# Decays of two heads in one tile, and in-block matmuls that alternate between the column halves of the array

## The chip, the cores and the metric

The kernel runs on one core of a Trainium2 chip. The metric is the device time of one execution in microseconds (us). TensorE (PE) multiplies matrices, VectorE (DVE), ScalarE (ACT) and GpSimd (POOL) work elementwise, and SyncE (SP) mainly issues DMA transfers. Each engine takes its instructions in the order of its own queue and waits on semaphores for the others.

## What is computed

The reference is one residual block over 512 tokens and 2048 channels: a root-mean-square norm, one wide projection, a retention branch (8 heads), a Mamba-2 branch (SSD, 64 heads of 64 channels in 8 groups), a gated merge, an output projection and a final norm. The change lies in the scan of the SSD branch. Cut to that:

```python
acum = jnp.cumsum(ac, axis=1)
seg = acum[:, :, None] - acum[:, None, :]
decay = jnp.exp(jnp.where(causal, seg, -jnp.inf))
cb = jnp.einsum('blgn,bsgn->blsg', cc, bc)
y = jnp.einsum('blsg,blsgh,bsghp->blghp', cb, decay, xc)
y = y + jnp.einsum('blgn,bghpn->blghp', cc, state) * jnp.exp(acum)[..., None]
```

`cb` belongs to a group and is shared by its 8 heads; `decay` belongs to a head. The product with `decay`, summed over the tokens `s` of a block, is what this text calls the in-block sum.

## The kernel before

The 512 tokens (T) are four blocks (TB) of 128 (P). Most of the time goes to the projections: `unit` makes 256 output columns for all tokens. Its float32 operands are split into two parts of reduced precision (`split`, L150 and L151), so that each product takes three matmuls (L202 to L204). SP loads the weights `wf` (L216), DVE forms sums of weight blocks (L219 to L222), ACT makes the high part `whi`, DVE the low part `wlo`. PE accumulates in the PSUM banks `pb`.

The scan's stage starts at L557. For each of 8 groups there is one unit for B and C, then twice (`jj`): a unit for x, a unit for z, the scan of two feature blocks (`e` = 0, 1), and a unit of the merge gates (`gates`, L582). A feature block is 128 channels, that is two heads. For each one:

- x is transposed and scaled (L621 to L627, `xd`, `xl`), the states at the block ends are formed (L630 to L639, `S`);
- for each of the two heads, SP loads the head's cumulative decay `A_d`, the same 512 numbers for all 128 partitions, into a tile `L` of two buffers (L644). ACT makes the decays with four Relus, one for each token block (L646), and one exponential (L648). DVE multiplies with `CB`, the group's masked `cb` (L649). Four matmuls (L651) form the in-block sums;
- these four use 64 weight columns each. The first head's result goes to PSUM partitions 0 to 63 and the second's to 64 to 127, so each head uses one column half of the array;
- three matmuls bring in the states (L655), and DVE and ACT finish `y` (L657 to L667).

The matmuls of L621, L630, L651 and L655 are float32 and leave two records each in the trace; those of L202 to L204 leave one. An unbroken run of L651 matmuls on PE is called a block below.

The order on each engine's queue is not that of the text. A scheduler of the framework (L819) lists the whole program with a model of times, so PE's scan matmuls stand among the projection matmuls of the next units.

Of the kernel before, what the change touches and what calls it, by code (L numbers as in the profile page):

```python
# [8 lines left out]
F32 = mybir.dt.float32  # L9
F32R = mybir.dt.float32r  # L10
I32 = mybir.dt.int32
AF = mybir.ActivationFunctionType
ALU = mybir.AluOpType
# [3 lines left out]
P = 128  # L17
T = 512
# [13 lines left out]

# columns of the constant array
C_ID, C_TRI, C_ONE, C_FREQ, C_END = 0, 128, 256, 384, 386


def _parts_of_inverse_two_pi():
    """1/(2 pi) as a sum of 12-bit pieces, high to low."""
    digits = 0.15915494309189533576888376337251436203445964574045644874766734405889
    from fractions import Fraction  # L40

    # 1/(2 pi) to 200 bits by Machin's formula
    def atan_inv(n, bits):
        one = 1 << bits
        term = one // n
        total, k, sign = term, 1, 1
        while term:
            term //= n * n
            k += 2
            sign = -sign  # L50
            total += sign * (term // k)
        return total

    bits = 240
    pi = 4 * (4 * atan_inv(5, bits) - atan_inv(239, bits))
    inv = Fraction(1 << bits, 2 * pi)
    assert abs(float(inv) - digits) < 1e-15
    parts = []
    for i in range(5):
        step = Fraction(1, 1 << (14 + 12 * i))  # L60
        n = inv // step
        parts.append(float(n * step))
        inv -= n * step
    return parts


def constants():
# [7 lines left out]
    for h in range(NH):  # L75
# [5 lines left out]

# A 256-row by 256-column block of weights B times a 256-feature by 512-token block of
# activations A.  Rows of A are the token halves, its columns the two feature tiles; t1 is
# half 1 and t0 is half 2, the odd weight tile is column 1 and the even one column 2.
# Activation slots: 0 A21, then A12-(A21+A22-A11), 1 A11, 2 A22, 3 A12, 4 A21+A22,
# 5 A21+A22-A11, 6 A21-A11.
# Weight slots: 0 B12, then B22+B11-B12, 1 B11, 2 B22, 3 B21, 4 B11-B12, 5 B22-B12,
# 6 B21-(B22+B11-B12).
# A product is (bank, half of the bank, weight slot, activation slot).
# SEVEN: Strassen's products in Winograd's form.  EIGHT: the block product with A21 as  # L90
# A11+(A21-A11), on the weights as they are.
SEVEN = (((0, 0, 1, 1), (1, 0, 3, 3), (1, 1, 0, 5)),
# [4 lines left out]
         ((2, 0, 0, 6), (2, 0, 2, 2), (2, 1, 2, 3)))  # L97
# EIGHT in two passes, the second half of the tokens first, each with banks of its own.
PASSES = ((((0, 0, 1, 1), (0, 1, 0, 1)), ((1, 0, 3, 3), (1, 1, 2, 3))),
# [12 lines left out]
class InOrder:  # L112
    """An engine whose instructions issue in the order of the program."""

# [15 lines left out]
def hybrid_block(tc, A, out):  # L130
# [15 lines left out]
    def att_tile():  # L146
        return att.tile([P, T], F32, name="att")
# [4 lines left out]

    # ------------------------------------------------ products with the weights
    def combined(f, eng):
# [7 lines left out]
    def operands(i, f):  # L162
        """The seven activation operands of feature pair i from its raw slots 0-3 in f."""
        combined(f, POOL if i in FORM_POOL else DVE)
# [12 lines left out]
    def load_operands(forms, src, last=None):  # L177
        """Operands of 2048 features of a DRAM array [features, T]; the last pair may be on chip."""
        H = []
# [9 lines left out]
    def products(H, parts, pt, groups, PE=PE, after=None):  # L189
        """The products of groups, for 256 columns of weights, into the banks pt: parts are  # L190
        DRAM arrays [2048, n], side by side."""
        started, ws = set(), []
# [46 lines left out]
    def unit(H, parts, alt=False, plain=False):  # L239
        """W^T A for 256 columns of weights as two tiles [128, T], feature-major."""  # L240
        nb = 3 if plain else 4
# [21 lines left out]

    # ---------------------------------------------------------------- stage 0
    cc = cst.tile([P, C_END], F32, name="cc")
# [8 lines left out]

    # scratch
    yr_d = dp.tile([D, T], F32, name="yr_d")
# [12 lines left out]
    def inverse_root(dst, ps, y, z, n, DVE=DVE, ACT=ACT):  # L289
        """dst = (ps / n + eps) ** -0.5 for sums in PSUM; a Newton step makes it exact.  # L290
        y, z: room for one tile each."""
        ACT.activation(y, ps, AF.Abs_reciprocal_sqrt, scale=1.0 / n, bias=eps)
# [4 lines left out]

    # forms of the activations before they are split: A8 and B8 serve other ends between
    bg_ctx = ExitStack()
# [15 lines left out]
    with tc.tile_pool(name="st0", bufs=1) as st:  # L315
        def early(tag):
            """Room of an operand that is not yet there."""
            return hp.tile([P, 7 * 256], F32, name=f"e_{tag}", tag=tag)

        # the order of the arithmetic here is that of the text  # L320
        pe, act, dve, pool = (InOrder(tc, e) for e in (PE, ACT, DVE, POOL))
        raw = [early(f"hl{i}")[:, :2 * T].rearrange("p (r t) -> p r t", r=2) for i in range(NP)]
        wdt = early("hh7")[:, :KD * SH].rearrange("p (k c) -> p k c", k=KD)
        for i, x in enumerate(raw):
            SP.dma_start(out=x, in_=rows(A["xT"], i))
            if i == 0:
                SP.dma_start(out=cc, in_=A["consts"])
        # brings the table in ahead
        act.activation(rstd[:, :1], eps, AF.Abs_reciprocal_sqrt)
# [27 lines left out]

        # the normalized activations
        fs, hs, H = {}, {}, []
# [25 lines left out]
    def rotary_tables(positions, x):  # L385
        """cos and sin of the angles, which are rounded as the reference rounds them, then
        counted in turns and reduced exactly; x is room for four tiles."""
        turn, a1, a2, ki = (x[:, i, :] for i in range(4))
# [34 lines left out]
    def step_sizes(v, pool):  # L423
        """dt = softplus(h w + bias), the cumulative decays in blocks of 128 tokens."""
        u, w, s, s2 = (v[:, i, :].rearrange("p (c h) -> p c h", c=TB) for i in range(4))
# [8 lines left out]
        for tb in range(TB):  # L434
            DVE.scalar_tensor_tensor(u[:, tb, :], pt[:, tb * SH:(tb + 1) * SH], rstd[:, tb:tb + 1], dtb,
                                     op0=ALU.mult, op1=ALU.add)
        # softplus: max(u, 0) + log1p(exp(-|u|)), log1p(w) = 2 atanh(w / (2 + w))
        DVE.tensor_scalar(w, u, -1.0, None, op0=ALU.mult)
# [36 lines left out]

    # -------------------------------------------------------------- retention
    with tc.tile_pool(name="ret", bufs=1) as rp:
# [3 lines left out]
        for h in range(NH):  # L481
            # the decays stay where the gate comes later
            dec = sg[:, 0, :]
# [72 lines left out]

    # -------------------------------------------------------------------- SSD  # L557
    with tc.tile_pool(name="ssd", bufs=1) as sp:
        # conv taps and bias; D
        cw = sp.tile([P, 48, 5], F32, name="cw")  # L560
# [12 lines left out]
        def conv(x, j, dst):  # L573
            """causal convolution over tokens and SiLU of one feature block."""
            ACT.activation(dst, x, AF.Identity, scale=cw[:, j, 3:4], bias=cw[:, j, 4:5])
# [13 lines left out]
        for g in range(NG):  # L589
# [14 lines left out]
            for jj in range(2):  # L604
# [5 lines left out]
                for e in range(2):  # L610
# [5 lines left out]
                    for i in range(2):  # L616
                        SP.dma_start(out=E[i * 64:(i + 1) * 64, :], in_=E_d[h0 + i, P:].partition_broadcast(64))
                    # x token-major, scaled by dt, and by dt and the decay to the block's end
                    ps = att_tile()
# [14 lines left out]
                    for c in range(1, TB - 1):  # L634
                        for i in range(2):
# [3 lines left out]
                                                     op0=ALU.mult, op1=ALU.add)  # L639
                    pi = att_tile()  # L640
                    for i in range(2):
                        # decay from s to l within a block; s > l is zeroed by CB
                        L = sp.tile([P, TB, P], F32, name="L", bufs=2)
                        SP.dma_start(out=L.rearrange("p c l -> p (c l)"), in_=A_d[h0 + i].partition_broadcast(P))  # L644
                        for c in range(TB):
                            ACT.activation(L[:, c, :], L[:, c, :], AF.Relu, scale=-1.0,  # L646
                                           bias=At[:, c, h0 + i:h0 + i + 1])
                        ACT.activation(L, L, AF.Exp, scale=-1.0)  # L648
                        DVE.tensor_tensor(L, L, CB, op=ALU.mult)  # L649
                        for c in range(TB):  # L650
                            PE.matmul(pi[i * 64:(i + 1) * 64, c * P:(c + 1) * P], xd[:, c, i, :], L[:, c, :],  # L651
                                      start=True, stop=True)
# [19 lines left out]

    # --------------------------------------------------- branch projections
    with tc.tile_pool(name="br", bufs=1) as bp:
# [41 lines left out]

    # ----------------------------------------------------- output projection
    with tc.tile_pool(name="fin", bufs=1) as fp:
# [16 lines left out]

        # the last two feature blocks, the odd one first, half of the tokens after the other
        t = xo[NP - 1]
# [85 lines left out]
```

## Time and profile before

| | |
|---|---|
| median of 3 runs | 2796.94 us |
| lowest, highest | 2796.71, 2799.17 us |
| span of the profiled execution | 2798.7 us (no other time is given for it) |
| PE busy | 2738.8 us, 98% of the span |
| DVE busy | 2380.8 us, 85% |
| ACT busy | 1333.9 us, 48% |
| in-block matmuls L651, busy | 59.5 us, 512 records |

The span runs from the first to the last instruction of one execution. Busy time is the union of an engine's instructions; matmuls overlap each other in the pipeline, so a record's duration (0.28 us) is longer than the step from one start to the next. "Idle before" is the time in which an engine had nothing to do ahead of the instructions of a group, and what ended it. PEld is the load of weights into the array.

### The profile page before, as it was taken

The page shows a single profiled execution, that of the slowest core. Times are in us where ns is not written, and L with a number is a line of the kernel's source. Part 1 is how long each engine was busy: PE and PEld are TensorE (multiplying, and loading weights), DVE is VectorE, ACT ScalarE, POOL GpSimd, SP SyncE. Part 2 cuts the span into 40 slices and gives each one's busy share as a digit, 9 for nine tenths or more (in the row PEclk, how much of TensorE's full clock was granted, in tenths as well). Part 3 has the DMA queues.
Part 4 walks back from the last instruction along what each step waited for, and adds up shares of the span by engine and source line. Part 5 has one row for each costly group of instructions (what it writes and reads, how often), then busy time and mean ns, then how long its engine had stood idle before and what let it go on. Part 6 is the DMA issues. An engine that isn't in the chain of part 4 may idle for free.

```text
span 2798.7 us, 55732 instructions
## 1 busy us (share of the span) xinstructions
PE 2738.8 (98%) x22236; PEld 2680.0 (96%) x22236; DVE 2380.8 (85%) x3746; ACT 1333.9 (48%) x1885; POOL 254.1 (9%) x206
## 2 busy tenths in 40 slices
PE   7999999999999999999999999999999999999898
PEld 4999999999999999999999999999999999999898
DVE  8998888888879888888888888888888798788997
ACT  4434333333345655564655555555553343433443
POOL 4000000000000000000000000000020030111311
PEclk9999999999999999999999999999999999999999
DMA  3333333333333444343443434334455554566634
GB/s 124 106 97 101 102 102 103 110 92 109 102 104 119 127 134 127 108 137 108 127 125 121 135 121 135 104 118 128 124 187 165 167 180 130 166 184 190 220 105 139
DMA packets 344388, 362.69 MB, mean 130 GB/s; under 512 B 25664, under 2 KB 298304, under 8 KB 344128
## 3 DMA queue, kind: packets, MB, share of 16 engines
q1 hardware_dynamic: 323888, 325.32, 38.5%
q10 hardware_dynamic: 20240, 33.82, 3.3%
q8 instruction: 174, 2.85, 0.4%
q14 instruction: 86, 0.70, 0.1%
HBM read 321.56 MB, written 37.49 MB: 128 GB/s over the span
## 4 chain that ended last, share of the span: by engine, by line
PE 82%; DVE 7%; DMA 6%; issue 3%; POOL 1%; ACT 1%; SPq 0%; DVEq 0%; ACTq 0%; POOLq 0%
PE pb L203 22%; PE pb L202 22%; PE pb L204 22%; PE att L204 2%; PE att L202 2%; PE att L203 2%; PE att L651 2%; DVE wlo L151 2%; DMA wf<-in_w_in_dram 2%; PE att L537 1%; PE att L522 1%; DMA wf<-in_w_br_ssd_dram 1%; PE att L655 1%; PE pb L120 1%; PE att L630 1%
## 5 line engine op out<-in xcount | busy, mean ns | idle before, releaser
L203 PE MATMUL pb<-hl,whi 128*128 128x256 f32 x5944 | 1686.5, 285 | 10.8 <-DVE hl L120 6.0
L202 PE MATMUL pb<-hh,whi 128*128 128x256 f32 x5944 | 1685.7, 285 | 6.2 <-ACT hh L150 3.2
L204 PE MATMUL pb<-hh,wlo 128*128 128x256 f32 x5944 | 1673.5, 284 | 3.7 <-DVE wlo L151 3.6
L150 ACT CAST whi<-wf 128x896 fp32r<-128x896 f32 (+1 forms) x968 | 822.1, 885 | 873.9 <-PE pb L203 414.8
L203 PEld LDWEIGHTS pb<-hl,whi 128*128 128x128 f32 x5944 | 1141.9, 192 | 17.6 <-DVE hl L120 6.9
L202 PEld LDWEIGHTS pb<-hh,whi 128*128 128x128 f32 x5944 | 1139.3, 192 | 10.2 <-ACT hh L150 3.6
L204 PEld LDWEIGHTS pb<-hh,wlo 128*128 128x128 f32 x5944 | 1136.0, 192 | 5.5 <-DVE wlo L151 5.1
L151 DVE TENSOR_TENSOR wlo<-wf,whi 128x896 fp32r<-128x896 f32 (+1 forms) x968 | 997.4, 1040 | 78.6 <-PE pb L204 25.9
L219 DVE TENSOR_TENSOR wf<-wf 128x512 f32<-128x512 f32 x404 | 286.3, 709 | 168.1 <-DMA wf<-in_w_in_dram 114.3
L204 PE MATMUL att<-hh,wlo 128*128 128x256 f32 x864 | 241.8, 285 | 7.8 <-DVE wlo L151 7.8
L202 PE MATMUL att<-hh,whi 128*128 128x256 f32 x864 | 245.4, 285 | 1.4 <-ACT whi L150 1.4
L203 PE MATMUL att<-hl,whi 128*128 128x256 f32 x864 | 244.8, 285 | 0.0
L221 DVE TENSOR_TENSOR wf<-wf 128x256 f32<-128x256 f32 x404 | 182.8, 454 | 4.3
L204 PEld LDWEIGHTS att<-hh,wlo 128*128 128x128 f32 x864 | 165.1, 193 | 8.8 <-DVE wlo L151 8.8
L222 DVE TENSOR_TENSOR wf<-wf 128x256 f32<-128x256 f32 x404 | 170.7, 424 | 3.2
L202 PEld LDWEIGHTS att<-hh,whi 128*128 128x128 f32 x864 | 167.6, 194 | 1.8 <-ACT whi L150 1.6
L203 PEld LDWEIGHTS att<-hl,whi 128*128 128x128 f32 x864 | 167.5, 194 | 0.0
L626 POOL TENSOR_TENSOR xl<-xd,sst 128x384 f32<-128x384 f32 x32 | 33.6, 1049 | 876.9 <-DVE xd L623 819.7
L646 ACT ACTIVATE L<-L,sst 128x128 f32<-128x128 f32 x256 | 80.1, 390 | 59.6 <-DMA L<-A_d 47.1
L256 ACT COPY o<-pb 128x256 f32<-128x256 f32 x89 | 32.9, 370 | 144.4 <-PE pb L204 137.2
L257 DVE TENSOR_TENSOR o<-pb,o 128x512 f32<-128x512 f32 x89 | 60.9, 684 | 34.5 <-PE pb L204 34.2
L543 POOL TENSOR_TENSOR rs<-rs,mhalf 128x1 f32<-128x1 f32 x32 | 24.9, 784 | 709.5 <-DVE rs L542 700.2
(230 smaller groups left out, 2113.1 us busy)
## 6 DMA issues: line engine op xcount, KB each, us to landing
wf<-in_w_in_dram SPq DMA_DIRECT2D x640, 256.0 KB, 3.1
wf<-in_w_br_ssd_dram SPq DMA_DIRECT2D x128, 256.0 KB, 3.6
wf<-in_w_out_dram SPq DMA_DIRECT2D x72, 256.0 KB, 3.2
wf<-in_w_in_dram SPq DMA_DIRECT2D x128, 128.0 KB, 2.6
L<-A_d SPq DMA_DIRECT2D x64, 256.0 KB, 3.5
wf<-in_w_br_ret_dram SPq DMA_DIRECT2D x64, 256.0 KB, 3.7
ys_d<-B ACTq DMA_DIRECT2D x32, 256.0 KB, 2.8
E<-E_d SPq DMA_DIRECT2D x64, 96.0 KB, 3.0
```

The source lines that it names most:

```text
L150: ACT.copy(dst_hi, src)
L151: DVE.tensor_tensor(dst_lo, src, dst_hi.bitcast(F32), op=ALU.subtract)
L202: PE.matmul(o, wh, xh, start=b not in started, stop=False, skip_group_check=True)
L203: PE.matmul(o, wh, xl, start=False, stop=False, skip_group_check=True)
L204: PE.matmul(o, wl, xh, start=False, stop=(k == NP - 1), skip_group_check=True)
L219: DVE.tensor_tensor(f2[:, :, 4:6, :], f2[:, :, 1:3, :], f2[:, :, 0:1, :].to_broadcast([P, 2, 2, P]), op=ALU.subtract)
L221: DVE.tensor_tensor(f2[:, :, 0, :], f2[:, :, 2, :], f2[:, :, 4, :], op=ALU.add)
L222: DVE.tensor_tensor(f2[:, :, 6, :], f2[:, :, 3, :], f2[:, :, 0, :], op=ALU.subtract)
L257: DVE.tensor_tensor(o[:, 1:3, :], pt[1], p1[:, None, :].to_broadcast([P, 2, 256]), op=ALU.add)
L626: POOL.tensor_tensor(xl, xd[:, :TB - 1], tail[:, :TB - 1, hs, None].to_broadcast([P, TB - 1, 2, 64]), op=ALU.mult)
L646: ACT.activation(L[:, c, :], L[:, c, :], AF.Relu, scale=-1.0, bias=At[:, c, h0 + i:h0 + i + 1])
L651: PE.matmul(pi[i * 64:(i + 1) * 64, c * P:(c + 1) * P], xd[:, c, i, :], L[:, c, :], start=True, stop=True)
```

## The change

The two heads of a feature block share one tile `L` of 128 x 2 x 4 x 128, in one buffer instead of two of half the size (the pool's default is one). One DMA brings both heads' decays, the eight Relus stay, and there is one exponential and one multiplication with `CB` for both heads. The in-block matmuls go over token blocks outside and heads inside, so that neighbours write to different column halves. All other lines of the diff remove comments and document strings.

```diff
                     pi = att_tile()
+
+                    L = sp.tile([P, 2, TB, P], F32, name="L")
+                    SP.dma_start(out=L.rearrange("p i c l -> p i (c l)"),
+                                 in_=A_d[hs, :].partition_broadcast(P))
                     for i in range(2):
-                        # decay from s to l within a block; s > l is zeroed by CB
-                        L = sp.tile([P, TB, P], F32, name="L", bufs=2)
-                        SP.dma_start(out=L.rearrange("p c l -> p (c l)"), in_=A_d[h0 + i].partition_broadcast(P))
                         for c in range(TB):
-                            ACT.activation(L[:, c, :], L[:, c, :], AF.Relu, scale=-1.0,
+                            ACT.activation(L[:, i, c, :], L[:, i, c, :], AF.Relu, scale=-1.0,
                                            bias=At[:, c, h0 + i:h0 + i + 1])
-                        ACT.activation(L, L, AF.Exp, scale=-1.0)
-                        DVE.tensor_tensor(L, L, CB, op=ALU.mult)
-                        for c in range(TB):
-                            PE.matmul(pi[i * 64:(i + 1) * 64, c * P:(c + 1) * P], xd[:, c, i, :], L[:, c, :],
+                    ACT.activation(L, L, AF.Exp, scale=-1.0)
+                    DVE.tensor_tensor(L, L, CB[:, None].to_broadcast([P, 2, TB, P]), op=ALU.mult)
+
+                    for c in range(TB):
+                        for i in range(2):
+                            PE.matmul(pi[i * 64:(i + 1) * 64, c * P:(c + 1) * P], xd[:, c, i, :], L[:, i, c, :],
                                       start=True, stop=True)
```

The scheduler lists the stage anew, and what moves is shown at three places. In the changed kernel L647 is the Relu, L649 the exponential, L650 the multiplication, L654 the in-block matmul and L658 the matmul with the states; L643 is the load.

PE, the second feature block of a pair (group 1, first pair), before:

```order
L202 MATMUL pb_11359<-hh_277,whi 128x256
L651 MATMUL att<-L,xd 64x128 x4
L203 MATMUL pb_11359<-hl_290,whi 128x256
L204 MATMUL pb_11359<-hh_277,wlo 128x256
L202 MATMUL pb_11359<-hh_277,whi 128x256
L655 MATMUL att<-A_8779,S 128x128
L651 MATMUL att<-L,xd 64x128 x4
L203 MATMUL pb_11359<-hl_290,whi 128x256
```

and now:

```order
L202 MATMUL pb_11337<-hh_266,whi 128x256
L203 MATMUL pb_11337<-hl_284,whi 128x256
L654 MATMUL att<-L,xd 64x128 x8
L658 MATMUL att<-A_8779,S 128x128 x2
L204 MATMUL pb_11337<-hh_266,wlo 128x256
```

The two blocks of four matmuls have become one of eight. In all there are 17 rows of "x8" and 30 of "x4" before, and 32 rows of "x8" now. From the end of the first feature block's row to the second's there are 60 projection matmuls and 10 float32 ones here before, and 94 and 10 now (77 and 10, and 96 and 10, in the pairs that come second in their group).

ACT, the decays of the second feature block of a pair (group 1, second pair), before:

```order
L646 ACTIVATE L<-L,sst 128x128 x8
L150 CAST whi<-wf 128x896
L648 ACT_TABLE_LOAD
L648 ACTIVATE L<-L 128x512
L150 CAST whi<-wf 128x896
L648 ACTIVATE L<-L 128x512
```

and now:

```order
L647 ACTIVATE L<-L,sst 128x128 x8
L150 CAST whi<-wf 128x896 x2
L649 ACT_TABLE_LOAD
L649 ACTIVATE L<-L 128x1024
```

Two casts of weights now stand between the Relus and the exponential of both heads. Further on, the exponential of the next pair's first feature block stands behind the Sigmoids of the gates (L585) and has a table load of its own; the order has 17 table loads at the exponential before and 30 now.

SP, the loads of the decays around the same place, before:

```order
L644 DMA L<-A_d 128x512 x2
L216 DMA wf<-in_w_in_dram 128x2x128 x4
L617 DMA E<-E_d 64x384 x2
L216 DMA wf<-in_w_in_dram 128x2x128 x4
L644 DMA L<-A_d 128x512 x2
```

and now:

```order
L643 DMA L<-A_d 128x1024
L216 DMA wf<-in_w_in_dram 128x2x128 x4
L617 DMA E<-E_d 64x384 x2
L216 DMA wf<-in_w_in_dram 128x2x128 x4
L643 DMA L<-A_d 128x1024
```

The place among the weight loads stays; one issue stands where two stood. The order changes from the start of the scan's stage up to its seam with the branch projections (the first loads of L185 and L681 on SP among them); behind that no row of any engine changes its place.

## Rows read from the trace of the kernel before

**Rows 1.** The page's head: span, and each engine's busy time.

```profile
span 2798.7 us, 55732 instructions
PE 2738.8 (98%) x22236; PEld 2680.0 (96%) x22236; DVE 2380.8 (85%) x3746; ACT 1333.9 (48%) x1885; POOL 254.1 (9%) x206
```

**Rows 2.** Busy time in the scan's stage: engines in order, granted clock, DMA share, GB/s.

```profile
800.00:2080.00 1280.00, 1275.52 (x10636) 1259.52 (x10635) 1085.71 (x1719) 722.95 (x1131) 86.70 (x71) 1.00 0.42 126
```

**Rows 3.** Groups by line and shape: busy us, mean ns, idle before.

```profile
L651 PE MATMUL att<-L,xd 128*64 128x128 f32 x512 | 59.5, 279 | 0.4 <-DVE L L649 0.4
L151 DVE TENSOR_TENSOR wlo<-wf,whi 128x896 fp32r<-128x896 f32 x808 | 880.6, 1098 | 56.7 <-ACT whi L150 20.6 <-PE pb L204 19.9 <-ACT L L646 7.4
...
L649 DVE TENSOR_TENSOR L<-L,A 128x512 f32<-128x512 f32 x64 | 48.6, 770 | 9.7 <-ACT L L648 9.6
...
L648 ACT ACTIVATE L<-L 128x512 f32<-128x512 f32 x64 | 40.0, 627 | 0.2
...
L648 ACT ACT_TABLE_LOAD x17 | 21.8, 1283 | 0.3
...
L250 ACT COPY o<-pb 128x1024 f32<-128x1024 f32 x15 | 15.2, 1014 | 22.0 <-PE pb L204 22.0
```

**Rows 4.** Timeline of PE, first block of 16 records: start us, us, instruction.

```profile
863.38 1.58 PE L651 MATMUL att<-L,xd 128*64 128x128 f32 x16
864.89 0.39 PE L203 MATMUL pb<-hl,whi 128*128 128x256 f32 x1
865.12 0.28 PE L204 MATMUL pb<-hh,wlo 128*128 128x256 f32 x1
```

**Rows 5.** Timeline of PE, first block of 8 records.

```profile
873.69 0.28 PE L204 MATMUL pb<-hh,wlo 128*128 128x256 f32 x1
873.81 0.28 PE L202 MATMUL pb<-hh,whi 128*128 128x256 f32 x1
874.02 1.09 PE L651 MATMUL att<-L,xd 128*64 128x128 f32 x8
875.03 0.39 PE L203 MATMUL pb<-hl,whi 128*128 128x256 f32 x1
875.26 0.28 PE L204 MATMUL pb<-hh,wlo 128*128 128x256 f32 x1
```

**Rows 6.** L651 alone, two windows inside the block of Rows 4: PE, PEld.

```profile
863.60:863.85 0.25, 0.25 (x4) 0.25 (x3) 1.00 0.00 0
...
864.25:864.50 0.25, 0.25 (x8) 0.25 (x4) 1.00 0.00 0
```

**Rows 7.** Timeline of all engines, from a pair's first block to its second.

```profile
1232.54 1.58 PE L651 MATMUL att<-L,xd 128*64 128x128 f32 x16
...
1233.65 0.83 SPq L644 DMA_DIRECT2D L<-A_d  x2
...
1236.92 2.46 ACT L646 ACTIVATE L<-L,sst 128x128 f32<-128x128 f32 x8 [0.20 <-DMA L<-A_d]
...
1239.29 0.93 ACT L150 CAST whi<-wf 128x896 fp32r<-128x896 f32 x1
...
1242.19 0.69 DVE L649 TENSOR_TENSOR L<-L,A 128x512 f32<-128x512 f32 x1 [0.27 <-ACT L L648]
...
1244.40 1.78 DVE L649 TENSOR_TENSOR L<-L,A 128x512 f32<-128x512 f32 x1
...
1245.23 1.09 PE L651 MATMUL att<-L,xd 128*64 128x128 f32 x8
```

**Rows 8.** DMA issues: KB each, median us from issue to landing.

```profile
L<-A_d SPq DMA_DIRECT2D x64, 256.0 KB, 3.5
...
e_hl<-in_xT_dram SPq DMA_DIRECT2D x8, 512.0 KB, 7.8
...
A<-ys_d SPq DMA_DIRECT2D x6, 512.0 KB, 4.0
...
B<-yr_d SPq DMA_DIRECT2D x3, 512.0 KB, 5.3
```

## The prediction

> **What bounds the kernel now.** I read the page's head first: TensorE (PE) is busy for 98% of a span of 2798.7 us, the next engine for 85% [rows 1]. Then the busy time by stage. In the scan's stage, 800 to 2080 us, PE is busy for 1275.5 of 1280 us; VectorE (DVE) for 1085.7 and ScalarE (ACT) for 723.0 [rows 2]. The granted clock is 1.00 there, the 2.4 GHz level, so there is no clock to win back. PE waits in this stage for 4.5 us in all; what counts is therefore how long PE needs for the work in its queue, and whether anything newly comes too late for it.
>
> The grouped rows give the size of what is changed: 512 records of the in-block matmul (L651) with 59.5 us of busy time, after 0.4 us of idle [rows 3]. Each float32 matmul leaves two records, so 512 records are 8 for each of 64 heads.
>
> Then I read single stretches of PE, and here lies the argument. Where the 8 matmuls of a feature block stand together, 16 records take 1.58 us [rows 4]. Where one head's four stand alone, 8 records take 1.09 us [rows 5], so one after another they start every (1.09 - 0.28) / 7 = 0.116 us. Sixteen in single file would take 1.09 + 8 x 0.116 = 2.02 us, not 1.58. The windows inside one such block say where the 0.44 us went: 0.25 us early in the block touches 4 records, 0.25 us in its middle touches 8 [rows 6]. In the middle, where the last records of the first head (column half 0) and the first of the second (half 1) are in the queue together, **both halves run at once, each at its own pace**. At the ends of the block only one half has work near the head of the queue.
>
> **The change part by part.**
> 1. *What a block costs PE today.* From the start of a block to the second instruction behind it is 865.12 - 863.38 = 1.74 us for 16 records [rows 4] and 875.26 - 874.02 = 1.24 us for 8 [rows 5]. Of this 0.12 is the ordinary step of the first follower (taken by the two neighbours, 873.69 to 873.81), and the step into the block is 0.21 instead of 0.12 [rows 5], 0.09 more. So a block of 16 costs 1.71 us, one of 8 costs 1.21 us. The order of before has 17 blocks of 16 and 30 of 8 (17 rows of "x8" and 30 of "x4"). Their busy time by the single rows, 17 x 1.58 + 30 x 1.09 = 59.6 us, agrees with 59.5 [rows 3]. Cost: 17 x 1.71 + 30 x 1.21 = **65.4 us**.
> 2. *What it costs afterwards.* All 32 blocks have 16 records, and the halves alternate from one matmul to the next. What bounds it: at best the second half runs wholly beside the first, and a block lasts as long as 8 records do today, 1.21 us, plus 0.01 for the later start: 32 x 1.22 = 39.0 us, 26.4 less. The other end is today's block of 16 with no better overlap: 32 x 1.71 = 54.7 us, 10.7 less. I take the first. In the middle of today's block the other half already runs although three matmul records of the first half stand between them in the queue; with alternation one stands between. Term: **-26.4 us**.
> 3. *Merged ACT and DVE work.* 64 exponentials of 0.627 become 32 of 1024 columns, which I price like the 128x1024 copy, 1.01: 40.1 to 32.4 us. The order shows 30 table loads for them instead of 17, 13 x 1.283 = 16.7 us more [rows 3]. ACT gains 9 us of work and has 557 us idle in the stage [rows 2]. 64 multiplications of 0.770 become 32 of 1.098 x 1024 / 896 = 1.25: 49.3 to 40.0 us of DVE [rows 3], which has 194 us idle [rows 2]. Neither is on PE's path except through item 4. If that cover were gone, they would cost up to 9 us on ACT and give 9 on DVE.
> 4. *The late chain, and queues.* The second feature block of each pair needs its L after the first block has released it. Today the load is issued 1233.65 - 1232.54 = 1.11 us into the first block, when head 0 is done; eight Relus (2.46), a cast (0.93), the table load, the first exponential and a multiplication follow, the first multiplication starts at 1242.19 and the second head's at 1244.40, and PE takes the blocks at 1245.23 and later [rows 7]. Afterwards one load of 512 KB waits for the whole block, which is itself shorter (8-record length, about 1.0 us), so it is issued at the same 1.1 us. It lands after 4.0 us: the bounds are 3.5, as the halves do, and 5.3, the slower mid-kernel row of 512 KB [rows 8]. Then 2.46 + two casts 1.86 + 1.28 + 1.01 + 1.25: ready 13.0 us into the first block, 12.5 at best, 15.4 at worst (with a 1.1 us DVE operation ahead). PE comes to it after 1.0 + 96 x 0.12 + 20 x 0.116 = 14.8 us, since the order now has 96 projection matmuls and 10 float32 ones between the two blocks (77 and 10 before). Slack 1.8 us, at worst -0.6, which would be 16 x 0.6 = 10 us. Behind the waiting load on SP's queue stand the same weight loads as before, and one issue in place of two; its bytes are the same. On DVE the merged multiplication holds up the weight splits behind it while it waits for the exponential; today's such waits are 9.7 us [rows 3]. The single L buffer delays nothing else: in front of the next pair's first block the order has at least 409 projection matmuls (237 in the first group), 28 us or more. I put all new waits at **+2 us**, about half of the 4.5 that PE waits now [rows 2].
>
> Sum: -26.4 + 2 = -24.4 us, so the profiled span of 2798.7 becomes 2774.3. That span is 1.8 us above the median of the runs, 2796.9; against the median the forecast is **2772.5 us**.
>
> *A rule that speaks against it.* The windows show 8 records of two column halves in the time in which 4 of one half run [rows 6]. The Trainium skill, page "TensorE: Matmul & The Clock Gate", section "The mechanism" (under packing small matmuls), says that weight loads overlap with running matmuls only where the row group differs, and that matmuls start and end strictly in order. Both halves here use all 128 rows, so by that rule they would run in single file; it is rival C. The same page, section "Measured speedup vs the span model", gives 2.38 times for three column tiles; an estimate from that figure, at the same efficiency per tile, is 1.59 times for two, a block of about 1.4 us and a gain of some 19 us.
>
> **The rivals.**
> - *A, full overlap*, as summed: 2772.5. For it: rows 4 to 6.
> - *B, no more overlap than today*, because the look-ahead of the queue and not the order limits it: 10.7 less plus 2, 2788 at most, 2786 without new waits. Against it: the order of today puts the halves as far apart as possible.
> - *C, single file:* 32 x (1.21 + 8 x 0.116) = 68.4, 3.0 more than today: 2800, within the noise. Against it: today's 16-record block takes 1.58 and not 2.02 us.
> - *D, the late chain*, the side that ends slower: the place is the merged load in front of each pair's second block, 16 times. If the load lands after 7.8 us, as the 512 KB loads at the start of the kernel do [rows 8], the chain is 3.8 us longer than summed and PE waits 3.8 - 1.8 = 2.0 us each time: 16 x 2.0 = 32 us against 26.4 gained, 2803. It eats the whole gain at 26.4 / 16 = 1.65 us of waiting and shows as a loss from 2.0 us on. Against it: the halves land in 3.5 us today, with the same bytes in flight, and those 7.8 us fall where eight such loads start together.
> - *E, each change of half drains the array:* the edges of a block cost 0.09 on entry and 0.23 - 0.12 = 0.11 on exit [rows 5]; seven changes in a block at 0.20 make 32 x (2.14 + 1.4) = 113 us, 48 more: 2845. Against it: the one change inside today's block costs nothing.
>
> **How the numbers follow.** A 0.72, B 0.12, C 0.05, D 0.08 (half of it only eats the gain), E 0.03. The predicted time is A's. The low end, 2766, is full overlap with today's 4.5 us of waits gone as well (2796.9 - 26.4 - 4.5); the high end, 2788, takes in B with its waits and A with the 10 us of the late end of item 4. What can be told from no change here is about 0.2%, 5.6 us. Faster: A and B, 0.84. Within: C and half of D, 0.09. Slower: the other half of D and E, 0.07.
>
> **What would show it.** In the profile after: 32 blocks of 16 records of the in-block matmul, each about 1.1 us in the timeline, 35 us of busy time in the group instead of 59.5; 8 records in every 0.25 us of a block; the ends of the stage earlier by some 24 us and everything behind it only shifted; the 512 KB load landing in 3.5 to 5.3 us; PE waiting for the merged multiplication not at all or for a few tenths. Blocks of 1.6 us would speak for B, of 2 us for C, of over 3 us for E; a PE idle time of over 1.5 us in front of each pair's second block for D.

## The result and the profile after

The changed kernel takes 2782.08 us (median of 4 runs, 2779.75 to 2783.91), the kernel before 2796.82 us beside it (4 runs): a ratio of 0.9943, 95% interval 0.9929 to 0.9957, that is 14.7 us less. It lies within the predicted range and on the predicted side, 9.6 us above the predicted time. Measured twice more, each time with fresh runs of the kernel before, the same program gave 0.9915 (0.9901 to 0.9929; 23.3 us less) and 0.9925 (0.9911 to 0.9939; 20.5 us less). One of the eleven runs of the kernel before beside the third measurement was a slow one of 4741.98 us and is left out of its median, 2797.01 us. The forecast was 24.4 us less.

The page's head answers to [rows 1]; the profiled run took 2783.91 us:

```profile
span 2782.1 us, 55602 instructions
...
PE 2717.0 (98%) x22236; PEld 2659.9 (96%) x22236; DVE 2378.8 (86%) x3714; ACT 1342.8 (48%) x1866; POOL 257.9 (9%) x206
```

TensorE has 21.8 us less work in a span that is 16.6 us shorter. The difference is new idle time, and the next views look for it. First the groups that answer to [rows 3] (L654 is the in-block matmul, L649 the exponential and its table loads, L650 the multiplication, L219 a sum over weights, of which more below):

```profile
L219 DVE TENSOR_TENSOR wf<-wf 128x512 f32<-128x512 f32 x404 | 287.0, 711 | 168.5 <-DMA wf<-in_w_in_dram 115.1 <-DMA wf<-in_w_br_ssd_dram 31.8 <-DMA wf<-in_w_br_ret_dram 12.9
...
L650 DVE TENSOR_TENSOR L<-L,A 128x1024 f32<-128x1024 f32 x32 | 45.7, 1429 | 14.2 <-ACT L L649 14.2
...
L649 ACT ACT_TABLE_LOAD x30 | 38.5, 1283 | 0.5
...
L654 PE MATMUL att<-L,xd 128*64 128x128 f32 x512 | 35.0, 279 | 0.8 <-issue 0.4
...
L649 ACT ACTIVATE L<-L 128x1024 f32<-128x1024 f32 x32 | 33.9, 1059 | 0.4
```

The in-block matmuls are down from 59.5 to 35.0 us of busy time, the same 512 records of the same 279 ns each. The timeline of TensorE shows the first block, to be set beside [rows 4] and [rows 5]:

```profile
862.17 1.09 PE L654 MATMUL att<-L,xd 128*64 128x128 f32 x16
863.20 0.39 PE L203 MATMUL pb<-hl,whi 128*128 128x256 f32 x1
863.42 0.28 PE L204 MATMUL pb<-hh,wlo 128*128 128x256 f32 x1
```

Sixteen records now last as long as eight did, 1.09 us, and from the block's start to its second follower it is 1.25 us where eight records took 1.24. Two windows inside this block, L654 alone (PE, PEld as in [rows 6]):

```profile
862.20:862.45 0.25, 0.25 (x6) 0.25 (x7) 1.00 0.00 0
862.40:862.65 0.25, 0.25 (x8) 0.25 (x6) 1.00 0.00 0
```

Eight records in 0.25 us is what the kernel before reached only in the middle of a block.

So the array gave what was summed, and the rest must be waiting. Busy time from 800 to 2045 us, the part of the stage that lies within the scan in each kernel, before and after (PE, PEld, DVE, ACT, POOL, clock, DMA share, GB/s):

```profile
800.00:2045.00 1245.00, 1240.52 (x10342) 1224.82 (x10341) 1058.18 (x1679) 701.50 (x1099) 75.66 (x62) 1.00 0.41 123
```

```profile
800.00:2045.00 1245.00, 1234.02 (x10473) 1219.87 (x10472) 1066.81 (x1668) 721.43 (x1101) 84.97 (x64) 1.00 0.41 125
```

TensorE's idle time there is 1245 - 1240.5 = 4.5 us before and 11.0 us after. The last in-block record starts at 2038.2 us where it started at 2052.8, 14.6 us earlier instead of the 24 forecast. The waits of TensorE in that stretch of the changed kernel say for whom (us in all, times, longest):

```profile
PE pb L202 <- DVE o L259: 5.6, 7, 1.8
PE att L658 <- DVE S L637: 2.1, 4, 1.0
PE att L600 <- ACT A L580: 1.6, 1, 1.6
PE pb L202 <- DVE o L257: 0.7, 2, 0.5
PE att L654 <- issue: 0.4, 1, 0.4
```

The longest wait is not for the decays. It is a projection matmul (L202) that needs a PSUM bank, which L259 on VectorE has yet to empty. VectorE's timeline around the longest of them:

```profile
1216.32 0.68 DVE L257 TENSOR_TENSOR o<-pb,o 128x512 f32<-128x512 f32 x1
1218.75 0.69 DVE L219 TENSOR_TENSOR wf<-wf 128x512 f32<-128x512 f32 x1 [1.75 <-DMA wf<-in_w_in_dram]
1219.36 0.68 DVE L258 TENSOR_TENSOR o<-o,pb 128x512 f32<-128x512 f32 x1
1219.96 1.08 DVE L151 TENSOR_TENSOR wlo<-wf,whi 128x896 fp32r<-128x896 f32 x1
1220.96 0.42 DVE L221 TENSOR_TENSOR wf<-wf 128x256 f32<-128x256 f32 x1
1221.30 0.41 DVE L259 TENSOR_TENSOR o<-o,pb 128x256 f32<-128x256 f32 x1
```

and TensorE's, same place:

```profile
1219.75 0.28 PE L202 MATMUL pb<-hh,whi 128*128 128x256 f32 x1
1221.86 0.35 PE L202 MATMUL pb<-hh,whi 128*128 128x256 f32 x1 [1.83 <-DVE o L259]
```

VectorE stands idle for 1.75 us at L219, the last of the four weight sums of the next unit of projection work, until its load lands. The evacuations L258 and L259 of the present unit are listed behind it, and TensorE needs them first. That order was there before the change: the last weight sum of the next unit stands ahead of L259 in 85 of the 101 units, before and after alike. The kernel before lost 0.8 us to L259 in this stretch, the changed one 5.6.

### The profile page after: what moved, and what is told of

It reads as the page before. It is cut to its first block, busy times and chain, and to the rows that moved or that the text cites. A ratio compares the mean times of both kernels' runs of the same rounds, so it can differ in the third digit from the quotient of the medians.

```text
span 2782.1 us, 55602 instructions
## 1 busy us (share of the span) xinstructions
PE 2717.0 (98%) x22236; PEld 2659.9 (96%) x22236; DVE 2378.8 (86%) x3714; ACT 1342.8 (48%) x1866; POOL 257.9 (9%) x206
## 4 chain that ended last, share of the span: by engine, by line
PE 80%; DVE 8%; DMA 6%; issue 3%; ACT 1%; POOL 1%; SPq 1%; DVEq 0%; POOLq 0%; ACTq 0%
PE pb L203 21%; PE pb L204 21%; PE pb L202 21%; PE att L204 3%; PE att L203 3%; PE att L202 3%; DMA wf<-in_w_in_dram 3%; DVE wlo L151 2%; PE att L537 1%; PE att L522 1%; PE att L654 1%; PE pb L120 1%; DVE wf L219 1%; DVE hl L151 1%; PE att L658 1%
## 5 line engine op out<-in xcount | busy, mean ns | idle before, releaser
L202 PE MATMUL pb<-hh,whi 128*128 128x256 f32 x5944 | 1687.4, 285 | 10.1 <-DVE o L259 5.6
L150 ACT CAST whi<-wf 128x896 fp32r<-128x896 f32 (+1 forms) x968 | 820.4, 886 | 943.5 <-PE pb L203 407.6
L202 PEld LDWEIGHTS pb<-hh,whi 128*128 128x128 f32 x5944 | 1140.7, 192 | 15.5 <-issue 8.4
L219 DVE TENSOR_TENSOR wf<-wf 128x512 f32<-128x512 f32 x404 | 287.0, 711 | 168.5 <-DMA wf<-in_w_in_dram 115.1
L202 PE MATMUL att<-hh,whi 128*128 128x256 f32 x864 | 244.1, 284 | 1.1 <-ACT whi L150 1.1
L202 PEld LDWEIGHTS att<-hh,whi 128*128 128x128 f32 x864 | 166.5, 193 | 1.5 <-ACT whi L150 1.5
L626 POOL TENSOR_TENSOR xl<-xd,sst 128x384 f32<-128x384 f32 x32 | 34.2, 1069 | 855.3 <-DVE xd L623 798.5
L647 ACT ACTIVATE L<-L,sst 128x128 f32<-128x128 f32 x256 | 78.5, 389 | 32.7 <-DMA L<-A_d 32.4
```

The costliest lines, as they stand in the source:

```text
L150: ACT.copy(dst_hi, src)
L202: PE.matmul(o, wh, xh, start=b not in started, stop=False, skip_group_check=True)
L219: DVE.tensor_tensor(f2[:, :, 4:6, :], f2[:, :, 1:3, :], f2[:, :, 0:1, :].to_broadcast([P, 2, 2, P]), op=ALU.subtract)
L626: POOL.tensor_tensor(xl, xd[:, :TB - 1], tail[:, :TB - 1, hs, None].to_broadcast([P, TB - 1, 2, 64]), op=ALU.mult)
L647: ACT.activation(L[:, i, c, :], L[:, i, c, :], AF.Relu, scale=-1.0, bias=At[:, c, h0 + i:h0 + i + 1])
```

## Experiments

Two theories stood against each other at first. Theory O: the new waits come from the order of VectorE's queue, now that TensorE arrives earlier, and would come with anything that makes TensorE faster there. Theory M: the merged tile makes them, since one larger load, exponential and multiplication hold up what stands behind. The runs of e1 to e4 share the kernel before at 2795.21 us, those of f1 to f4 at 2796.77 us, those of g1 to g3 at 2797.01 us; each of the three sets ran on a chip of its own. The changed kernel itself ran with the sets f and g but not with e, so the expectations of e1 to e4 start from the first result, 2782.08 us, which turned out to be the slowest of its three. Line numbers in the fences are those of each run's own kernel: where the rule of e4 is in, L208, L225, L588 and L609 are what L202, L219, L580 and L600 are in the changed kernel.

**e1: alternation without the merged tile.** Tiles, loads, exponentials and multiplications stay apart by head; the matmuls alternate.

```diff
-                    L = sp.tile([P, 2, TB, P], F32, name="L")
...
+                        L = sp.tile([P, TB, P], F32, name="L", bufs=2)
...
+                        Ls.append(L)
                     for c in range(TB):
                         for i in range(2):
-                            PE.matmul(pi[...], xd[:, c, i, :], L[:, i, c, :],
+                            PE.matmul(pi[...], xd[:, c, i, :], Ls[i][:, c, :],
```

> Alternation alone: each head keeps its own tile, load, exponential and multiplication as before the change; the four matmuls of the two heads alternate once both multiplications are done. All theories: 32 blocks of 16 records of 1.1 us, 35 us of busy time in the in-block group. Theory O (the missing 9 us are waits that come from how the queues are listed, above all DVE, where weight sums stand in front of the PSUM evacuations, and PE now runs ahead of them): new waits stay, 2776 to 2784 us. Theory M (the merged tile, its later load, longer exponential and extra table loads cause the waits): they vanish, 2770 to 2774 us.

2790.72 us, ratio 0.9981 (0.9972 to 0.999): both were missed. With separate tiles the scheduler cuts the second block of each pair into one matmul and seven:

```profile
874.81 0.43 PE L654 MATMUL att<-L,xd 128*64 128x128 f32 x2
...
876.66 1.09 PE L654 MATMUL att<-L,xd 128*64 128x128 f32 x14
```

The group costs 41.8 us instead of 35.0, and a wait that neither of the two kernels has appears, for the scaled values from POOL:

```profile
PE att L630 <- POOL xl L626: 6.9, 8, 1.1
```

So one tile per pair of heads does something after all: it lets the eight matmuls be listed as one block. e1 doesn't separate O from M, since its listing is another.

**e2: the merged tile without alternation.** The listing is that of the changed kernel; only the order of the eight matmuls differs.

```diff
-                    for c in range(TB):
-                        for i in range(2):
+                    for i in range(2):
+                        for c in range(TB):
```

> The merged tile, but the heads one after the other in the matmuls; every queue keeps the order of the changed kernel. Blocks last 1.58 us on the timeline as the blocks of 16 before the change, PE's work grows by 32 x 0.49 = 15.7 us against the changed kernel. Theory O: a slower PE is less ahead of DVE, so part of the 8.8 us of new waits goes and the time is 2790 to 2795 us. Theory M: the waits stay, 2796 to 2799 us. If the alternation were not what gives the gain: 2782 us.

2786.13 us, ratio 0.9967 (0.9954 to 0.9979), 9.1 less than before; the first block is at 1.58 us again. The waits for L259 are there without alternation:

```profile
PE pb L202 <- DVE o L259: 3.8, 5, 1.2
```

The time is below both ranges and above the 2782 us of no effect, so it decides nothing between O and M. By the prediction's prices the merge alone saves 65.4 - 32 x 1.71 = 10.7 us of blocks, and TensorE's idle time is 1245 - 1238.4 = 6.6 us, 2.1 more than before: 8.6, close to the 9.1 measured. The idle time lies among those of the changed kernel (11.0 us above, 5.5 and 7.3 in f1 and g1 below), whose VectorE has the same listing and whose TensorE is faster.

**e3: two token blocks of one head, then two of the other.** Again the same listing, with three changes of column half in a block instead of seven.

```diff
-                    for c in range(TB):
+                    for c0 in (0, 2):
                         for i in range(2):
+                            for c in (c0, c0 + 1):
```

> The changed kernel with two token blocks of one head, then two of the other, and so on: four records of one column half stand together in PE's queue instead of two. If the queue looks ahead past three waiting matmuls, as the overlap in the old blocks suggested, blocks last 1.1 us or up to 0.25 us more, 2782 to 2790 us. If only direct neighbours overlap, blocks last 1.5 us or more and the time is 2796 us or more.

2776.1 us, ratio 0.9931 (0.9917 to 0.9944), below the expected range, whose lower end was the first result. The block is as the first alternative has it, hardly longer than with strict alternation (L655 is the in-block matmul here):

```profile
861.84 1.15 PE L655 MATMUL att<-L,xd 128*64 128x128 f32 x16
```

The halves run together even when two matmuls of one half (four records) stand in front of the other half's. Strict alternation isn't needed for most of the gain: the 512 records are busy for 36.6 us, against 35.0 in the changed kernel and 50.5 in e2.

**e4: the weight sum behind the evacuation, in the whole kernel.** The last of a unit's four weight sums is listed behind the last evacuation of the unit before, by an order dependency without a wait of its own. Nothing else changes in the program; the scheduler lists it anew.

```diff
-                        DVE.tensor_tensor(f2[:, :, 4:6, :], ...)
+                        w0 = DVE.tensor_tensor(f2[:, :, 4:6, :], ...)
+                        if k == 6 and drained[0]:
+                            behind(w0, drained[0])
...
-                DVE.tensor_tensor(o[:, 2:4, :], pt[2], o[:, 2:4, :], op=ALU.add)
+                drained[0] = DVE.tensor_tensor(o[:, 2:4, :], pt[2], o[:, 2:4, :], op=ALU.add).ins.name
```

> The changed kernel with one rule for the order on DVE: the last of a unit's four weight sums stands behind the evacuations of the unit before it. Nothing is computed differently. Theory O: PE's waits for the evacuations (6.3 us in the scan's stage) go and the time falls by 4 to 8 us, to 2774 to 2778 us. Theory M: no effect, 2780 to 2784 us. If the weight sums are needed that early, PE waits for weights instead and the time rises.

2774.99 us, ratio 0.9927 (0.9915 to 0.994). That is within theory O's range, but by luck: the range was counted from 2782.08 us, and without any rule the changed kernel took 2773.45 and 2776.47 us in f1 and g1. In the stage all waits but one are gone (TensorE busy for 1243.7 of 1245 us), but behind the scan new ones come up, such as this one in the output projection, 1.1 us in the changed kernel:

```profile
L208 PE MATMUL att<-hh,whi 128*128 128x256 f32 x864 | 244.0, 285 | 4.9 <-ACT whi L150 4.9
```

The rule holds the sums back there too, and the casts (L150) work on what the sums leave. Without the rule behind the scan (f2) that wait is 1.4 us. Hence the rule in the scan's stage alone, in four kernels that ran together.

**f1: the changed kernel again.**

> The changed kernel once more, beside the three that follow: 0.993 to 0.996 of the kernel before, as in its first measurement (0.9943), and about 9 us of PE waits in the scan's stage over those of before.

2773.45 us, 0.9915 (0.9901 to 0.9929), which misses the expectation on the fast side. TensorE's idle time in 800 to 2045 us is 1245 - 1239.5 = 5.5 us, half of the first profile's, and the wait for L259 is smaller:

```profile
PE pb L202 <- DVE o L259: 3.8, 6, 1.3
```

**f2: the changed kernel with the rule in the scan's stage.**

```diff
-                        if k == 6 and drained[0]:
+                        if k == 6 and scan[0]:
```

> The rule of the run before it, last weight sum behind the evacuations, in the scan's stage alone. Theory O: from the first to the last in-block matmul 1160 us as there (1176 in the changed kernel), and behind it 744 us as in the changed kernel (752 with the rule everywhere): 2765 to 2770 us. If the rule did not cost anything behind the scan: the same 2775 us.

2764.97 us (2763.7 to 2766.1), ratio 0.9884 (0.9871 to 0.9898): 31.8 us less than before and 8.5 less than f1. It beats both kernels. Its waits in the stretch are one line:

```profile
PE att L609 <- ACT A L588: 1.5, 1, 1.5
```

and VectorE's idle time ahead of the weight sums, over the whole kernel, falls from 149.0 us in f1 (168.5 in the first profile) to 131.4 us:

```profile
L225 DVE TENSOR_TENSOR wf<-wf 128x512 f32<-128x512 f32 x404 | 285.0, 708 | 131.4 <-DMA wf<-in_w_in_dram 90.0 <-DMA wf<-in_w_br_ssd_dram 21.8 <-DMA wf<-in_w_br_ret_dram 13.6
```

The 8.5 us are more than the idle time that went, 5.5 - 1.5 = 4.0 us. Idle time understates a wait: a record lasts 0.28 us and the next one normally starts 0.12 us after it, so a wait of up to 0.16 us shows no idle time and a longer one shows 0.16 us too little. The stretch from the first in-block record to the last holds the same TensorE records in f1 and f2, in another order (first and last start at the end of each row, f1 first):

```profile
L654 PE MATMUL att<-L,xd x512: 272/273/323, 862.8 to 2032.2; 128*64 128x128 f32 x171
```

```profile
L663 PE MATMUL att<-L,xd x512: 272/273/323, 860.6 to 2020.9; 128*64 128x128 f32 x171
```

It lasts 1169.4 us in f1 and 1160.3 us in f2, where TensorE is never idle: 9.1 us of waiting, of which idle time shows 4.6 (5.5 less the 0.9 us of a wait ahead of the first block).

The merged tile with its larger load, exponential and multiplication is still there and the waits are gone, so it does not make them by itself. The new listing also has 17 table loads at the exponentials instead of 30, and that was not tested apart. But each of the 15 waits that the first profile names between 800 and 2045 us (10.4 of the 11.0 us) has, on VectorE, a weight sum in the 4.2 us before it that sat idle for its load (0.4 to 2.5 us). The two together show the first half of theory O, that the waits come from the order of VectorE's queue. The second half, that they grew because TensorE arrives earlier, is not shown: e2, with slow blocks and the same listing of VectorE, has them too (1183.9 us for the same stretch against 1175.8 in f4, so 8.1 us).

**f3: the kernel before with the same rule.** The edit is that of f2 on the kernel before.

> The kernel before with the same rule in the scan's stage. Its order now has 24 blocks of 16 records and 16 of 8, so in-block matmuls cost 24 x 1.71 + 16 x 1.21 = 60.4 us instead of 65.4, and PE waited only some 5 us there. Theory O (the waits are the price of a PE that runs ahead, which this one does not): 3 to 8 us less than before. If the rule by itself were worth what it gave the changed kernel with the alternation: 10 us less or more.

2787.55 us, ratio 0.9966 (0.9953 to 0.9978), 9.2 less than before. The new listing has 24 blocks of 16 records and 16 of 8, which at the prediction's prices is 60.4 us instead of 65.4; the one wait left is 1.5 us where there were 4.5. Together 8.0. The time falls between the two ranges; the rule saves the kernel before about as much as the changed one (8.5), but more than half of it by the blocks of the new listing.

**f4: f2 without alternation.** The order of the matmuls as in e2.

> Merged tile, rule of order in the scan, heads one after the other in the matmuls: differs from f2_drain_first_scan in the order of the eight matmuls alone. With hardly any waits left to hide in, the alternation shows its full size: 32 x 0.49 = 15.7 us over f2_drain_first_scan. If it came out as 5 us or less, as without the rule (2786.1 against 2782.1), the alternation would be worth only that.

2780.22 us, ratio 0.9938 (0.9926 to 0.9951). f4 and f2 have one listing and no more than one wait each, so their difference, 15.25 us, is the alternation by itself. By the prices of blocks it is 32 x (1.71 - 1.22) = 15.7 us. And f3 less f4, 7.3 us, is the merge with the listing that it brings: 60.4 - 54.7 = 5.7 us by blocks.

**g1: the changed kernel a third time.**

> The changed kernel once more, beside the next two. If its time hangs on how late the transfers land in a session, it lies somewhere between the two earlier results, 0.9915 and 0.9943 of before, and TensorE's waits in the scan's stage (800 to 2045 us) lie between 5 and 11 us; if the first result was a single odd session, it is 0.991 to 0.992 with waits of 5 to 6 us.

2776.47 us, 0.9925 (0.9911 to 0.9939), with 1245 - 1237.7 = 7.3 us of idle time in the stretch: between the two others, as the first of the two expectations has it. The loads of 256 KB of weights land in 3.0 us here and in f1, 3.1 in the first profile (median), those of 128 KB in 2.4 against 2.6. No run changed the time of landing alone, and why it differs stays open:

```profile
wf<-in_w_in_dram SPq DMA_DIRECT2D x640, 256.0 KB, 3.0
...
wf<-in_w_in_dram SPq DMA_DIRECT2D x128, 128.0 KB, 2.4
```

But at one place in the one listing TensorE's wait goes with the idle time of the weight sum on VectorE. In the first profile:

```profile
1538.73 0.69 DVE L219 TENSOR_TENSOR wf<-wf 128x512 f32<-128x512 f32 x1 [1.45 <-DMA wf<-in_w_in_dram]
...
1541.83 0.36 PE L202 MATMUL pb<-hh,whi 128*128 128x256 f32 x1 [1.21 <-DVE o L259]
```

and in f1:

```profile
1535.29 0.69 DVE L219 TENSOR_TENSOR wf<-wf 128x512 f32<-128x512 f32 x1 [0.67 <-DMA wf<-in_w_in_dram]
...
1538.39 0.36 PE L202 MATMUL pb<-hh,whi 128*128 128x256 f32 x1 [0.64 <-DVE o L259]
```

In g1 the two are 1.23 and 0.95 us.

**g2: alternation with separate tiles, and the rule.** e1 with the edit of f2.

> Alternation alone (tiles, loads, exponentials and multiplications of each head apart), with the weight sum put behind the evacuation in the scan's stage. The listing cuts each second block into one matmul and seven: 16 blocks of 16 records, 16 of 2 and 16 of 14. Sized from e1, where such blocks had 40.8 us of busy time against 35.0, and 16 more edges of 0.20 us: 5.8 + 3.2 = 9 us more than with the merged tile. If the merging acts through the number of blocks alone: f2 + 9 = 2774 us. If the merging saves or costs something beside that (9 us less work on VectorE, 9 us more on ScalarE): 2778 or more, or 2770 or less.

2781.82 us, 0.9946 (0.9932 to 0.9959), 16 us more than g3, which has the merged tile. The blocks were foreseen at 9 us and make 10: the 40.8 us of e1 in the expectation end at 2045 us, and its whole kernel has 41.8, as this one does. The time lies above the 2778 us of the last alternative, but not for the work on VectorE and ScalarE that it names. Most of the rest is the wait for POOL again, which I had left out (L639 and L635 are L630 and L626 of the changed kernel):

```profile
PE att L639 <- POOL xl L635: 4.6, 7, 1.1
```

TensorE's idle time is 1245 - 1237.0 = 8.0 us against g3's 1.7. So 6.8 us of longer blocks, 3.2 of edges (forecast) and 6.3 of waiting make 16.3 of the 16.0.

**g3: a second rule on top of f2.** The multiplication of each pair's first block also goes behind the convolution on VectorE.

```diff
-                    DVE.tensor_tensor(L, L, CB[:, None].to_broadcast([P, 2, TB, P]), op=ALU.mult)
+                    t = DVE.tensor_tensor(L, L, CB[:, None].to_broadcast([P, 2, TB, P]), op=ALU.mult)
+                    if e == 0:
+                        tc.add_manual_dep(t.ins, conved[0], ...)
```

> The changed kernel with the weight sum behind the evacuation in the scan's stage, and besides the first block's decay multiplication of each pair behind the convolution on VectorE. TensorE has one wait of 1.5 us left in this stage, at the attention of the states, which neither order touches. If the waits were the only thing left to win there: 2765 us, no change against the kernel with the first rule alone (within 3 us). If VectorE's queue costs something that the waits do not show: 2760 or less.

2765.82 us, 0.9889 (0.9874 to 0.9904): no difference from f2. TensorE had one wait of 1.7 us left in this stage, and the second rule gave nothing.

## Why the prediction was right or wrong

- **Blocks today (item 1), right.** The price of 1.71 us for a block in single halves and 1.22 for an alternating one carried f4 against f2 to 0.5 us.
- **Full overlap (item 2), right to the size.** 32 blocks of 1.09 us, 35.0 us of busy time as predicted; a block costs 1.25 - 0.12 + 0.09 = 1.22 us. Reading two windows inside one block of the kernel before was enough for this term of -26.4 us.
- **ACT and DVE (item 3), hidden as said.** Exponentials and table loads went from 61.8 to 72.4 us on ScalarE (+10.6, forecast +9). The multiplications went from 48.6 to 45.7, not to 40.0: the median is 1226 ns as priced, but the longest lasts 2327 ns, and the mean is 1429.
- **The late chain (item 4), half right.** The load lands in 3.8 us (4.0 taken), but the chain ends later than the 13.0 us summed. One pair in rows, to be set beside [rows 7]:

```profile
1066.70 1.09 PE L654 MATMUL att<-L,xd 128*64 128x128 f32 x16
...
1067.84 0.34 SPq L643 DMA_DIRECT2D L<-A_d  x1
...
1071.56 2.45 ACT L647 ACTIVATE L<-L,sst 128x128 f32<-128x128 f32 x8 [1.15 <-DMA L<-A_d]
...
1076.99 1.06 ACT L649 ACTIVATE L<-L 128x1024 f32<-128x1024 f32 x1
...
1077.67 0.69 DVE L219 TENSOR_TENSOR wf<-wf 128x512 f32<-128x512 f32 x1 [0.96 <-DMA wf<-in_w_in_dram]
1078.28 1.08 DVE L151 TENSOR_TENSOR wlo<-wf,whi 128x896 fp32r<-128x896 f32 x1
1079.28 2.32 DVE L650 TENSOR_TENSOR L<-L,A 128x1024 f32<-128x1024 f32 x1
...
1081.70 1.09 PE L654 MATMUL att<-L,xd 128*64 128x128 f32 x16 [0.44 <-issue]
```

  The exponential is over at 1078.05, but VectorE is at a weight sum that sat idle for its load, does a weight split after it, and then needs 2.32 us for a multiplication that usually takes 1.23. It is done 14.9 us after the first block began, within the bounds of 12.5 to 15.4, and TensorE waited 0.44 us. The group's idle time is 0.8 us in all; the 16 x 0.6 us of the late end did not come. TensorE's way to the block was also summed a little too long: L621 leaves one record for each of its four matmuls and not two, so the ten float32 matmuls are 16 records and not 20, TensorE comes to the block after 14.4 us and not 14.8, and the slack was 1.4 us:

```profile
L621 PE MATMUL att<-cc,B 128*128 128x128 f32 x128 | 19.2, 272 | 0.0
```

- **The step that failed: "I put all new waits at +2 us".** By idle time they were +6.5 in the first profile (11.0 against 4.5), then +1.0 and +2.8. I had looked for new waits only where the edit stands, at L and its multiplication. I had seen that VectorE waits for weight loads, but did not ask what is listed behind such a wait and when TensorE needs it. The reserve between VectorE's evacuations and TensorE's next use of the bank was part of the cover of a faster block, and no term of mine priced it.

  Reading waits off idle time, as I did with the 4.5 us, also made them too small. Counted by the stretch from the first to the last in-block record, as under f2, the changed kernel waits for 1176.0 - 1160.3 = 15.7 us in the first profile (862.2 to 2038.2 us), 9.1 in f1 and 1172.0 - 1160.3 = 11.7 in g1 (863.5 to 2035.5). The kernel before takes 1189.4 us (863.4 to 2052.8) against 1179.9 in f3 (860.9 to 2040.8), of which 5.0 are blocks: some 4.5 us of waits, an estimate. The new waits are then 11.2, 4.6 and 7.2 us, and -26.4 with them gives -15.2, -21.8 and -19.2 for the measured -14.7, -23.3 and -20.5. With idle time alone it would be -19.9, -25.4 and -23.6. That the forecast of 24.4 came within 1.1 us of f1 doesn't bear out the +2: the waits there were more than twice that, and the interval of f1 runs from 19.9 to 27.7 us less.
- **The rivals.** B (1.7 us a block), C (2 us), E (over 3 us) fall with blocks of 1.09 us. C was read out of the Trainium skill, page "TensorE: Matmul & The Clock Gate", section "The mechanism", which says that weight loads overlap with running matmuls only where the row group differs. The single file is my conclusion from it and not the page's sentence, and the section itself also names a background weight buffer as a way to load ahead; the trace disagrees with the conclusion, with 16 records in the time of 8. The estimate from that page's 2.38 for three column tiles was too low as well: a block costs 1.22 us and not 1.4, and with 1.4 f4 and f2 would differ by 32 x (1.71 - 1.4) = 9.9 us and not by 15.25. D falls with 3.8 us of landing and 0.44 us of waiting.

## What to carry to other kernels

Two sets of small matmuls that write to different column halves of the array cost about as much as one set here (1.22 us a block against 1.21 for half as many), with one or two matmuls of a half in turn in the queue. One operand tile for both kept them together in this scheduler's listing. When such an edit makes the bounding engine faster, look on the engines behind it for an instruction that waits for a DMA it doesn't need yet, with an evacuation listed behind it. Here that order was worth 8.5 us, a third as much again as the edit itself in the same set of runs (23.3). And compare stretches with the same work, since idle time can show half of the waiting.

## What the runs showed of the hardware

The overlap of the halves reached further than the forecast needed: with two matmuls of one half ahead of the other half's (e3) a block still took 1.15 us, against 1.09 in strict alternation and 1.58 with four ahead (e2). And one program, run in three sets, had 11.0, 5.5 and 7.3 us of idle time in the same stretch of 1245 us and times of 2782.1, 2773.5 and 2776.5 us, while the kernel before stayed within 2796.77 to 2797.01 beside it. The spread is in the waits, not in the work, and at the place shown under g1 it goes with how long a weight sum sits idle for its load. Why the loads land later in one set is not known; the sets f and g ran on different chips, and that of the first is not on record.
